# A transformer layer's differential attention: softmaxes combined unnormalized, the head norm's squares in one float32 product, the gate guard on GpSimd

## The chip, the cores and the metric

One core of one Trainium2 chip runs the whole layer. The metric is the device time of one execution in microseconds. Five engines work side by side, each on its own queue in order: the tensor engine (PE, its weight loads PEld), VectorE (DVE), ScalarE (ACT), GpSimd (POOL) and the queue that issues the transfers (SP).

## The reference

One layer for one sequence of 1024 tokens with 1024 features, all in float32. Its parts that matter here are these.

```python
proj = h @ w_in                       # queries, keys, values, latents, gate path g
p_d = jax.nn.softmax(logit_d, axis=-1)            # 4 heads, two softmaxes each
attn_d = p_d[:, 0] - lam * p_d[:, 1]
o_d = jnp.einsum('bhqk,bkhd->bqhd', attn_d, dv)
o_d = _rms_norm(o_d, diff_sub_norm) * (1.0 - lam_init)   # over the 128 values of a head
out = (mixed * jax.nn.silu(g)) @ w_out
return x + gate[:, None, :] * out
```

The four differential heads subtract a second softmax, times a scalar lambda, from the first, and normalize the result per head by its mean square plus an eps of 1e-6. Four more heads are ordinary softmax attention (MLA). Attention is causal by chunks of 64 tokens. The concatenated heads are multiplied by silu of the gate path before the output projection.

## The kernel before, in words

The kernel keeps float32 accuracy on the tensor engine by splitting each operand into a high part in a reduced-precision float32 format and a low remainder, and adding three products (`mm3`, lines 61 to 65). It runs in stages: a prologue that normalizes and transposes x, the projections (about 70 to 290 us), the mixing of both kinds of attention (about 290 to 612 us) and the output projection.

The mixing, `mixing` (line 1117), walks over 32 steps, one per head and pair of query tiles of 128 rows: 16 differential ones (`d`), 16 MLA ones (`m`), with the last differential and first MLA steps interleaved. A step first makes the softmax tiles of its pair (`diff_probs`, line 1032) and then, one step behind, the transposes, the product with the values and the output of the pair before (`diff_out`, line 1056). The head norm of that output (`diff_norm`, line 1070) is put off to the next step. Between them gate tiles fill the tensor engine (`gate_tile`, line 790): six at the start of step 0 and one in each of steps 0 to 9, 16 in all. Each is 24 matmuls of 512 columns into one PSUM bank; then VectorE clamps it from below (798), ScalarE takes exp, log of one plus it and exp again (799 to 801), VectorE multiplies by the tile (802) and SP stores it to DRAM (803).

In `diff_probs` each query tile has two score tiles. VectorE evicts the negated scores from PSUM with their running minimum (`scores`, 962), ScalarE takes the exponentials with their row sums (972). VectorE inverts both sums (1049) and multiplies the second by minus lambda (1050), GpSimd scales the second tile (1051), and VectorE scales the first and adds the second (1052). The blended tile is transposed (1019), split into high and low parts on ScalarE and VectorE (1020, 1021) and multiplied with the values (63 to 65).

In `diff_out` ScalarE copies the product (1060) and squares it in reduced precision (1063), GpSimd squares it in float32 (1066) and takes the difference to ScalarE's (1067). In `diff_norm` two matmuls with a matrix of ones sum both over the 128 values (1077), ScalarE takes log and exp for the inverse root (1079, 1080), VectorE scales (1081), GpSimd multiplies by the gate tile, which is loaded from DRAM (1074, 1082), and ScalarE and GpSimd split the result (1083, 1085) for the store (1087).

The order of each engine's instructions isn't written out in the mixing: a planner with a cost model of its own orders them by priority when the program is built, and adds the semaphores. Loads of weights and values are also split into high and low parts on ScalarE and on VectorE or GpSimd (785, 786, 877, 878). Line 939 is a small memset on GpSimd in the MLA steps, line 824 a float32 product with ones in the projections.

## Time and profile before

| | us |
|---|---|
| median of 3 runs | 677.12 (676.3 to 678.02) |
| profiled execution, its own time | 675.18 |
| its span, first to last instruction | 673.2 |
| tensor engine busy | 636.0 |

The profile is one execution recorded by the hardware. Times in it count from the span's start. A busy time is the union of an engine's instructions; a matmul's end is modelled, so the streaming of matmuls shows in the distance of their starts. The idle time before an instruction is put down to the one that released it.

### The profile page before, as it was taken

What the parts mean: (1) busy time and instruction counts of PE and PEld (TensorE: products, weight loads), DVE (VectorE), ACT (ScalarE), POOL (GpSimd) and SP (SyncE); (2) the same over time, 40 slices, a digit from 0 to 9 for tenths busy, and PEclk for the clock granted to TensorE, in tenths of its full rate; (3) what the DMA queues carried; (4) which work ended last, traced back from release to release, by engine and by line L of the source; (5) the groups of instructions that cost most, each with busy time, mean ns of one, the idle gap of its engine ahead of it and who ended that gap; (6) DMA issues with size and microseconds to landing.
All of it is one profiled execution on the core that took longest, in us unless ns stands there. A gap on an engine that the chain in (4) does not pass through costs nothing.

```text
span 673.2 us, 11178 instructions
## 1 busy us (share of the span) xinstructions
PE 636.0 (94%) x3579; PEld 538.7 (80%) x3579; DVE 480.0 (71%) x1296; ACT 341.3 (51%) x820; POOL 282.5 (42%) x376
## 2 busy tenths in 40 slices
PE   6899998999999999989999989997999899999996
PEld 4578886878888888877888878886988788888885
DVE  5855899699987554635876867989976466367654
ACT  4433663744565344345766766877775344236200
POOL 2022415483355135304443544558655225349400
PEclk9999999999999999999999998998999999999999
DMA  9984152598657455499556385493365944514223
GB/s 323 304 203 127 41 172 58 148 286 263 185 144 217 120 162 148 133 237 291 139 151 188 98 241 132 137 289 123 95 188 169 300 144 134 148 46 126 80 111 113
DMA packets 115140, 112.97 MB, mean 168 GB/s; under 512 B 7712, under 2 KB 86614, under 8 KB 115072
## 3 DMA queue, kind: packets, MB, share of 16 engines
q1 hardware_dynamic: 114784, 112.12, 57.4%
q8 instruction: 30, 0.49, 0.3%
q14 instruction: 38, 0.31, 0.2%
q0 software_dynamic: 288, 0.05, 0.1%
HBM read 77.51 MB, written 34.62 MB: 167 GB/s over the span
## 4 chain that ended last, share of the span: by engine, by line
PE 62%; DVE 14%; DMA 11%; issue 4%; ACT 3%; POOL 3%; SPq 2%; DVEq 0%; POOLq 0%; ACTq 0%
PE lg L953 8%; PE u L63 7%; PE u L65 7%; PE u L64 7%; PE o L65 4%; PE o L63 4%; PE o L64 4%; PE pt L1019 3%; DVE p L962 3%; DMA raw<-mk_d 2%; PE acc L64 2%; PE acc L65 2%; PE acc L63 2%; PE u L392 2%; DMA dk<-dk_d 2%
## 5 line engine op out<-in xcount | busy, mean ns | idle before, releaser
L972 ACT ACTIVATE p<-p,mx 128x128 f32<-128x128 f32 (+7 forms) x96 | 74.3, 775 | 35.4 <-DVE p L967 19.2
L63 PE MATMUL u<-wh,hTh 128*128 128x512 f32 x192 | 75.8, 398 | 3.3 <-DVE xn L561 2.6
L65 PE MATMUL u<-wh,hTl 128*128 128x512 f32 x192 | 76.3, 397 | 0.0
L64 PE MATMUL u<-wl,hTh 128*128 128x512 f32 x192 | 75.7, 394 | 0.0
L962 DVE TENSOR_SCALAR_CACHE_REDUCE p<-lg 128x512 f32<-128x512 f32 (+5 forms) x96 | 52.6, 563 | 13.3 <-PE pt L1019 4.5
L953 PE MATMUL lg<-dk,dq 128*128 128x512 f32 (+2 forms) x192 | 52.2, 368 | 5.6 <-DVE p L962 3.3
L535 POOL TENSOR_TENSOR wl<-wraw,wh 128x512 fp32r<-128x512 f32 (+1 forms) x20 | 26.5, 1329 | 65.4 <-ACT wh L534 60.7
L63 PE MATMUL u<-hTh,wh 128*128 128x512 f32 x128 | 51.5, 402 | 0.0
L65 PE MATMUL u<-hTh,wl 128*128 128x512 f32 x128 | 51.0, 399 | 0.0
L64 PE MATMUL u<-hTl,wh 128*128 128x512 f32 x128 | 50.5, 394 | 0.0
L1019 PE MATMUL pt<-ident_r,p 128*128 128x128 f32 x288 | 45.9, 276 | 3.4 <-DVE pTl L1021 1.7
L63 PEld LDWEIGHTS u<-wh,hTh 128*128 128x128 f32 x192 | 36.1, 188 | 10.6 <-DVE xn L561 3.3
L65 PEld LDWEIGHTS u<-wh,hTl 128*128 128x128 f32 x192 | 36.1, 188 | 7.2 <-issue 0.4
L64 PEld LDWEIGHTS u<-wl,hTh 128*128 128x128 f32 x192 | 36.1, 188 | 6.7
L953 PEld LDWEIGHTS lg<-dk,dq 128*128 128x128 f32 x192 | 31.4, 195 | 11.3 <-DVE p L962 6.1
L1021 DVE TENSOR_TENSOR pTl<-pt,pTh 128x512 fp32r<-128x512 f32 x48 | 32.9, 688 | 10.6 <-ACT pTh L1020 10.2
L1107 POOL TENSOR_SCALAR p<-p,sm 128x128 f32<-128x128 f32 (+7 forms) x32 | 25.7, 806 | 34.7 <-DVE sm L1106 34.1
L1052 DVE SCALAR_TENSOR_TENSOR p<-p,sm,p 128x128 f32<-128x128 f32 (+7 forms) x32 | 33.1, 1040 | 9.7 <-POOL p L1051 9.7
L1019 PEld LDWEIGHTS pt<-ident_r,p 128*128 128x128 f32 x288 | 34.2, 141 | 6.4 <-DVE p L1052 2.5
L1020 ACT CAST pTh<-pt 128x512 fp32r<-128x512 f32 x48 | 27.5, 581 | 21.0 <-PE pt L1019 20.6
L1051 POOL TENSOR_SCALAR p<-p,sm 128x128 f32<-128x128 f32 (+7 forms) x32 | 25.5, 797 | 27.6 <-DVE sm L1050 10.6
L953 PE MATMUL lg<-mkh,mq 128*128 128x512 f32 (+2 forms) x96 | 34.0, 365 | 0.7 <-ACT mq L877 0.7
(321 smaller groups left out, 1913.8 us busy)
## 6 DMA issues: line engine op xcount, KB each, us to landing
wraw<-in_w_in_dram SPq DMA_DIRECT2D x40, 256.0 KB, 3.4
ada<-in_ada_w_dram SPq DMA_DIRECT2D x32, 256.0 KB, 6.6
dq<-dq_d SPq DMA_DIRECT2D x16, 512.0 KB, 6.9
xt<-in_x_dram SPq DMA_DIRECT2D x8, 512.0 KB
dk_d<-st SPq DMA_DIRECT2D x16, 256.0 KB
adag<-in_ada_w_dram SPq DMA_DIRECT2D x16, 256.0 KB
dq_d<-st SPq DMA_DIRECT2D x16, 256.0 KB, 3.1
sg_d<-sgt SPq DMA_DIRECT2D x16, 256.0 KB, 4.7
```

What stands on the lines that cost most here:

```text
L63: t.matmul(out, wh, xh, start=start, stop=False)
L64: t.matmul(out, wh, xl, start=False, stop=False)
L65: t.matmul(out, wl, xh, start=False, stop=stop)
L535: (nc.gpsimd if pool else nc.vector).tensor_tensor(l, raw, h.bitcast(F32), op=ALU.subtract)
L953: self.last_mm = nc.tensor.matmul(lg[:, :w], q, k, start=j == 0, stop=j == len(ops) - 1 and not add)
L962: nc.vector.tensor_scalar(o[:, :m], lg[:, :m], 1.0, mx if c0 else None, op0=ALU.mult, op1=ALU.min, accum_out=mx)
L972: nc.scalar.activation(p, p, AF.Exp, bias=mx, scale=-1.0, accum_out=sm)
L1019: nc.tensor.transpose(t[:, j * P : j * P + P], ptiles[e[1]][:, e[0] * P : e[0] * P + P], self.ident)
L1020: nc.scalar.copy(h[:, lo:512], t[:, lo:512])
L1021: nc.vector.tensor_tensor(l[:, lo:512], t[:, lo:512], h[:, lo:512].bitcast(F32), op=ALU.subtract)
L1052: v.scalar_tensor_tensor(pp[0], pp[0], sm[:, 0:1], pp[1], op0=ALU.mult, op1=ALU.add)
L1107: nc.gpsimd.tensor_scalar(p, p, sm[:, 0:1], 0.0, op0=ALU.mult, op1=ALU.add)
```

## The change

It changes three places. In the gate tile VectorE's clamp from below goes; ScalarE takes the first exponential straight from PSUM, and GpSimd clamps the exponential from above before the log. In the softmax blend the tiles stay unnormalized: the first tile is no longer scaled, and the second is scaled by minus lambda times the ratio of the sums within VectorE's blend; GpSimd's scaling of the tile goes, and GpSimd writes the squared first sum times 128 eps into one column. In the head norm ScalarE's squares stay in float32; GpSimd builds two diagonal matrices of those columns (128x128 each), adds them to the squares, and one float32 product with ones takes the place of the two reduced-precision ones, so that eps is scaled by the squared sum; the log no longer adds eps.

```diff
--- before.py
+++ after.py
@@ -31,7 +31,7 @@
 W1 = 7
 MID = 4
 BANKS = {"a": 2, "b": 3, "c": 2, "t": 1}
-GMIN = -88.0
+EMAX = 1.6e38
 FIRST = "acactc"
 FILL = (1, 1, 1, 1, 1, 1, 1, 1, 1, 1, 0, 0)
 STAGES = {"st": 2, "mst": 3}
@@ -795,8 +795,8 @@
             hi, lo = unit[k // 4]
             self.mm3(t, hi[:, k % 4], lo[:, k % 4], self.hTh[:, k, ts], self.hTl[q][k], k == 0, k == KT - 1)
         st = self.wp.tile([P, 512], F32, name="sgt", tag="wraw", bufs=WRAW)
-        v.tensor_scalar(st, t, GMIN, None, op0=ALU.max)
-        a.activation(st, st, AF.Exp, scale=-1.0)
+        a.activation(st, t, AF.Exp, scale=-1.0)
+        self.nc.gpsimd.tensor_scalar(st, st, EMAX, 0.0, op0=ALU.min, op1=ALU.max)
         a.activation(st, st, AF.Ln, bias=self.ones[:, 0:1])
         a.activation(st, st, AF.Exp, scale=-1.0)
         v.tensor_tensor(st, st, t, op=ALU.mult)
@@ -1030,9 +1030,11 @@
         return acc[:, 0:256]
 
     def diff_probs(self, opnd, h, pr):
+
         nc, v, ap = self.nc, self.nc.vector, self.ap
         kT, qT, bias = opnd
         ptiles = []
+        s2 = ap.tile([P, 2], F32, name="s2", tag="s2", bufs=6)
         for j in range(2):
             i = 2 * pr + j
             klen = S if self.general else (i + 1) * P
@@ -1046,40 +1048,41 @@
                 passes = lambda c0, w: [(q[:, x], kT[c][:, c0 : c0 + w]) for x in range(2)]
                 self.scores(passes, bias, gt, p, mx[:, c : c + 1], sm[:, c : c + 1], True)
                 pp.append(p)
-            v.reciprocal(sm, sm)
-            v.tensor_tensor(sm[:, 1:2], sm[:, 1:2], self.nlam, op=ALU.mult)
-            nc.gpsimd.tensor_scalar(pp[1], pp[1], sm[:, 1:2], 0.0, op0=ALU.mult, op1=ALU.add)
-            v.scalar_tensor_tensor(pp[0], pp[0], sm[:, 0:1], pp[1], op0=ALU.mult, op1=ALU.add)
+            r = sm[:, 1:2]
+            v.reciprocal(r, r)
+            v.scalar_tensor_tensor(r, sm[:, 0:1], self.nlam, r, op0=ALU.mult, op1=ALU.mult)
+            v.scalar_tensor_tensor(pp[0], pp[1], r, pp[0], op0=ALU.mult, op1=ALU.add)
+            nc.gpsimd.tensor_scalar(s2[:, j : j + 1], sm[:, 0:1], sm[:, 0:1], P * EPS, op0=ALU.mult, op1=ALU.mult)
             ptiles.append(pp[0])
-        return ptiles
-
-    def diff_out(self, vv, h, pr, ptiles):
+        return ptiles, s2
+
+    def diff_out(self, vv, h, pr, probs):
+        ptiles, s2 = probs
         pT = self.transpose_probs(pr, ptiles)
         acc = self.av(pT, vv)
         o = self.dp.tile([P, 256], F32, name="o", tag="o", bufs=3)
         self.nc.scalar.copy(o, acc)
-        hi = self.dp.tile([P, 256], F32R, name="sqd", tag="sqd", bufs=2)
-        lo = self.dp.tile([P, 256], F32R, name="sql", tag="sql", bufs=1)
-        self.nc.scalar.activation(hi, o, AF.Square)
-        g = self.nc.gpsimd
-        sq = self.dp.tile([P, 256], F32, name="sq", tag="sq", bufs=1)
-        g.tensor_tensor(sq, o, o, op=ALU.mult)
-        g.tensor_tensor(lo, sq, hi.bitcast(F32), op=ALU.subtract)
-        return lambda: self.diff_norm(h, pr, o, hi, lo)
-
-    def diff_norm(self, h, pr, o, hi, lo):
+        sq = self.dp.tile([P, 256], F32, name="sq", tag="sq", bufs=2)
+        self.nc.scalar.activation(sq, o, AF.Square)
+        dg = self.dp.tile([P, 256], F32, name="dg", tag="dg", bufs=1)
+        for j in range(2):
+            self.nc.gpsimd.tensor_scalar(dg[:, j * P : j * P + P], self.ident, s2[:, j : j + 1], 0.0, op0=ALU.mult, op1=ALU.add)
+        self.nc.gpsimd.tensor_tensor(sq, sq, dg, op=ALU.add)
+        return lambda: self.diff_norm(h, pr, o, sq)
+
+    def diff_norm(self, h, pr, o, sq):
         nc, v, a = self.nc, self.nc.vector, self.nc.scalar
         sl = slice(pr * 256, pr * 256 + 256)
         sg = self.dp.tile([P, 256], F32, name="sgs", tag="sgs", bufs=1)
         nc.sync.dma_start(sg, self.sg_d[h][:, sl])
         ms = self.bank("c", "ms")
-        for x in (hi, lo):
-            nc.tensor.matmul(ms[:, 0:256], self.ones_r, x, start=x is hi, stop=x is lo)
+        nc.tensor.matmul(ms[:, 0:256], self.ones, sq, start=True, stop=True)
         ms = ms[:, 0:256]
-        a.activation(ms, ms, AF.Ln, bias=self.eps_t, scale=1.0 / P)
+        a.activation(ms, ms, AF.Ln, scale=1.0 / P)
         a.activation(ms, ms, AF.Exp, scale=-0.5)
         v.scalar_tensor_tensor(o, o, self.gsub[:, 0:1], ms, op0=ALU.mult, op1=ALU.mult)
         nc.gpsimd.tensor_tensor(sg, o, sg, op=ALU.mult)
+        hi = self.dp.tile([P, 256], F32R, name="sqd", tag="sqd", bufs=2)
         a.copy(hi, sg)
         hi = hi.bitcast(F32)
         nc.gpsimd.tensor_tensor(o.bitcast(F32R), sg, hi, op=ALU.subtract)
```

## Rows read from the trace of the kernel before

**Rows 1.** The page's busy time of each engine, whole span (us, share of span, instructions).

```profile
PE 636.0 (94%) x3579; PEld 538.7 (80%) x3579; DVE 480.0 (71%) x1296; ACT 341.3 (51%) x820; POOL 282.5 (42%) x376
```

**Rows 2.** Busy time by stretch: stretch, length, engines (instructions), granted clock, DMA share, GB/s.

```profile
285.00:323.00 38.00, 35.29 (x164) 29.07 (x163) 18.17 (x55) 18.66 (x39) 9.86 (x15) 0.96 0.89 248
323.00:400.00 77.00, 75.98 (x450) 66.28 (x449) 61.77 (x170) 53.36 (x127) 34.49 (x41) 1.00 0.63 168
400.00:412.00 12.00, 10.32 (x55) 8.95 (x53) 7.19 (x19) 8.01 (x21) 4.26 (x7) 0.86 0.44 134
412.00:440.00 28.00, 28.00 (x164) 24.81 (x163) 25.23 (x59) 21.27 (x47) 16.76 (x19) 1.00 0.53 143
440.00:450.00 10.00, 9.27 (x71) 8.60 (x70) 8.28 (x23) 8.25 (x22) 4.99 (x10) 1.00 1.03 301
...
450.00:485.00 35.00, 31.27 (x189) 26.91 (x188) 32.31 (x103) 27.46 (x69) 26.98 (x33) 0.95 0.46 142
...
485.00:510.00 25.00, 23.95 (x167) 21.49 (x166) 20.98 (x71) 16.60 (x40) 14.01 (x22) 1.00 0.48 138
```

**Rows 3.** The chain that ended last, shares by line: first 412 to 450, then 450 to 485 us.

```profile
by line: DVE p L962 15.0%; issue 11.0%; DVE p L1052 9.6%; POOL p L1051 8.1%; DMA sgs<-sg_d 7.4%; POOL sgs L1082 4.8%; DVE lastl L1021 3.9%; POOL o L1085 3.7%; ACT p L972 3.6%; DVE mq L878 3.4%; DVE pTl L1021 3.4%; POOL vl L878 3.3%; PE u L6
...
by line: DVE p L962 23.1%; PE lg L953 18.1%; DVE p L1052 13.0%; issue 8.4%; DVE sm L1050 4.1%; DVE pTl L1021 3.8%; PE pt L1019 3.7%; ACT p L972 3.5%; DVE o L1081 3.2%; PE lg L956 3.1%; DVE p L967 2.3%; PE acc L63 2.1%; PE acc L64 2.0%; PE a
```

**Rows 4.** Costliest groups: count | busy us, mean ns | idle us before, releasers; first two all shapes.

```profile
L1051 POOL TENSOR_SCALAR p<-p,sm 128x128 f32<-128x128 f32 (+7 forms) x32 | 25.5, 797 | 27.6 <-DVE sm L1050 10.6
L1052 DVE SCALAR_TENSOR_TENSOR p<-p,sm,p 128x128 f32<-128x128 f32 (+7 forms) x32 | 33.1, 1040 | 9.7 <-POOL p L1051 9.7
...
L1050 DVE TENSOR_TENSOR sm<-sm,nlam 128x1 f32<-128x1 f32 x32 | 8.2, 257 | 0.5
...
L1051 POOL TENSOR_SCALAR p<-p,sm 128x512 f32<-128x512 f32 x4 | 2.8, 700 | 2.4 <-ACT sgt L800 2.1 <-DVE sm L1050 0.4
...
L1051 POOL TENSOR_SCALAR p<-p,sm 128x128 f32<-128x128 f32 x4 | 2.5, 628 | 0.5 <-ACT p L972 0.2 <-DVE sm L1050 0.2
...
L939 POOL MEMSET p<- 64x64 f32 x32 | 3.8, 147 | 13.1 <-PE pt L1019 13.0
```

**Rows 5.** Timeline near 402 us, GpSimd, then VectorE: start, length, instruction, idle time before.

```profile
401.04 0.74 POOL L1082 TENSOR_TENSOR sgs<-o,sgs 128x256 f32<-128x256 f32 x1 [5.51 <-DMA sgs<-sg_d]
...
402.27 1.03 DVE L1052 SCALAR_TENSOR_TENSOR p<-p,sm,p 128x256 f32<-128x256 f32 x1 [2.57 <-POOL p L1051]
```

**Rows 6.** Line 798: shortest, median and longest ns; first and last start in us.

```profile
L798 DVE TENSOR_SCALAR sgt<-u x16: 669/682/693, 276.4 to 442.7; 128x512 f32<-128x512 f32 x16
```

**Rows 7.** Costliest groups, the head norm's lines on GpSimd and the tensor engine.

```profile
L1066 POOL TENSOR_TENSOR sq<-o 128x256 f32<-128x256 f32 x16 | 11.4, 711 | 4.0 <-ACT o L1060 3.4 <-PE lg L953 0.6
...
L1067 POOL TENSOR_TENSOR sql<-sq,sqd 128x256 fp32r<-128x256 f32 x16 | 12.5, 779 | 3.9 <-ACT sqd L1063 2.0 <-issue 1.1 <-POOL p L1051 0.2
...
L1077 PE MATMUL ms<-sqd,ones_r 128*128 128x256 f32 x16 | 5.1, 317 | 2.3 <-ACT sqd L1063 2.1
...
L1077 PE MATMUL ms<-sql,ones_r 128*128 128x256 f32 x16 | 4.9, 308 | 0.4 <-POOL sql L1067 0.4
...
L1082 POOL TENSOR_TENSOR sgs<-o,sgs 128x256 f32<-128x256 f32 x16 | 12.1, 756 | 31.8 <-DVE o L1081 17.0 <-DVE sm L1050 7.5 <-DMA sgs<-sg_d 6.8
```

**Rows 8.** The chain's piece of one 256-column matmul; then the tensor engine's timeline near 275 us.

```profile
415.07 0.12 PE acc L65
...
274.71 1.02 PE L824 MATMUL gps<-gsum,ones_r 128*128 128x512 f32 x2
275.17 0.80 PE L65 MATMUL u<-hTh,wl 128*128 128x512 f32 x1
275.80 0.46 PE L724 MATMUL kqp<-ident_r,kk 128*128 128x128 f32 x4
```

**Rows 9.** Timeline near 457 us, GpSimd, then VectorE.

```profile
456.83 1.58 POOL L878 TENSOR_TENSOR vl<-raw,vh 128x512 fp32r<-128x512 f32 x1
...
457.20 1.22 DVE L1050 TENSOR_TENSOR sm<-sm,nlam 128x1 f32<-128x1 f32 x1
```

## The prediction

> **What bounds the kernel now.** I read the page first: the tensor engine is busy for 636.0 us of a span of 673.2 us [rows 1]. A change to the other engines can therefore only win the tensor engine's idle time, or time that it spends at the lower clock. Next I read the busy time by stretch, to see where that idle time is [rows 2]. The edited lines run from 276 us (the first gate guard) to about 510 us (the last head norm). From 285 to 510 us the tensor engine is idle for 38.00 - 35.29 = 2.71 us, then 1.02, 1.68, 0.00, 0.73, 3.73 and 1.05 us: 10.9 us in all. Two stretches also show a granted clock below 1. It is 0.86 over 12 us and 0.95 over 35 us, so a part of each ran at 1.2 instead of 2.4 GHz. At half speed the work lost is 12 x 0.14 = 1.7 us and 35 x 0.05 = 1.75 us. All that can be won here is thus some 14 us.
>
> Then the chain of work that ended last, for two stretches [rows 3]. From 412 to 450 us its largest parts are VectorE's score evictions (L962, 15.0%), the blend of two softmaxes on VectorE (L1052, 9.6%) and GpSimd's scaling of the second softmax (L1051, 8.1%). From 450 to 485 us VectorE leads (L962 23.1%, L1052 13.0%, L1050 4.1%) and no GpSimd scaling is among the first lines. VectorE is busy for 32.31 of those 35 us, more than the tensor engine with 31.27. So the idle time from 440 to 485 us hangs on VectorE, which the change relieves. In the first stretch, 285 to 323 us, the chain is loads of keys, which nothing here touches, and I count none of its 2.71 us.
>
> **The change part by part.** *Softmax blend.* Each of 32 query tiles loses GpSimd's scaling (25.5 us in all) and the handover in front of VectorE's blend, before which VectorE stood idle for 9.7 us waiting for that line [rows 4]. The blend itself stays: one pass over two tiles with one scalar, as before. The reciprocal shrinks from two columns to one and the one-column product becomes a one-column three-operand product; both are instructions on a column, so zero. The worst of these waits shows what else goes: GpSimd stands 5.51 us for the load of the gate tile in front of its product (L1082), the scaling is queued behind it, and VectorE's blend of a 256-wide tile starts 2.57 us late [rows 5]. After the change VectorE no longer depends on GpSimd's queue here. What is late next is the tensor engine's norm product, whose squares still wait for ScalarE behind that same gate product.
>
> *Gate guard.* Sixteen VectorE passes of 0.682 us over 128x512 go (10.9 us), the last at 442.7 us [rows 6]. In their place GpSimd does one pass over SBUF between ScalarE's first exponential and its logarithm. The nearest row is GpSimd's scaling of a 128x512 tile, 0.700 us [rows 4], so the length of a gate's own chain stays as it is (0.70 against 0.68) and I cost it at nothing. The cover is that 10 of the 16 gates come one per step, in a bank that is wanted again only a step later. If the cover goes, the price is in the rivals, because ScalarE's logarithm now waits with the score exponentials queued behind it. The first exponential now reads PSUM itself, which other ScalarE instructions here do as well: zero.
>
> By the Trainium skill (GPSIMD Engine Reference, Engine selection), an elementwise add, multiply or max over a tile belongs on VectorE, since GpSimd is about twice as slow with two inputs and roughly at line rate with one. The guard has one input, and the trace bears out the second half: 0.700 us against 0.682 us. Were the factor of two to hold for it, each guard would take some 0.7 us longer and the sum would come out up to 16 x 0.7 = 11 us worse, had all of it reached the tensor engine.
>
> *GpSimd's own load.* Gone are 25.5 us of scalings, 11.4 us of squares and 12.5 us of differences (49.4 us) [rows 4, 7]. Added are 16 guards at 0.70 (11.2), 32 one-column products between a memset's 0.147 and the 128x128 scaling's 0.628 us [rows 4], 32 diagonals of 128x128 at up to 0.628 (20), and 16 sums of 256 columns at 0.78 (12.5). I take the small products at 0.25 (8), being nearer to the memset, and the diagonals at 0.5 (16). That is 47.7 us: GpSimd is as busy as before, only at other places.
>
> *Norm product.* Two reduced-precision matmuls of 256 columns become one float32 product. The stream of such matmuls advances 0.12 us per 256 columns, so two take 0.24 [rows 8]. The trace has float32 products with the same ones, of 512 columns: the first starts at 274.71 us, an ordinary 512-column matmul follows, and the next instruction starts at 275.80. Of those 1.09 us the ordinary one takes 2 x 0.12, the product 0.85, so 256 columns take 0.43 [rows 8]. Each norm costs the tensor engine 0.19 us more, 3.0 us for 16. The lower end is zero, if it falls into idle time. About a third of the norms lie after 440 us, where there is some, so I take 2.0 us.
>
> *Its wait.* Before, the first matmul waits for ScalarE's square and the second for GpSimd's difference. The tensor engine stood still 2.3 and 0.4 us for them [rows 7]. Now the one product waits for GpSimd's sum, which follows the square and lasts 0.78 us (L1067's length), while the old first matmul covered 0.12 of that. Where the tensor engine waited for the square it now waits up to 0.66 us more. Behind the product in its queue stand score products and transposes. Bounds: zero (the planner places the product later) and 16 x 0.66 = 10.6 us. I take 0.5 us, nearer to zero, because L1077 waited but 2.7 us in 32 matmuls. The eps on the square sum only shifts a bias from ScalarE to the diagonal: zero.
>
> **The sum.** Won: from 440 to 485 us there are 0.73 + 3.73 = 4.46 us of idle time and 1.75 us of lost clock. VectorE reaches them earlier by the three guards after 412 us (2.0 us) and by its waits on GpSimd, so I take 4.0 of 6.2. From 400 to 412 us the gate load stays, so I take 1.0 of 3.4. From 323 to 400 and 485 to 510 us I take 0.5 each of 1.02 and 1.05. That is 6.0 us won, 2.5 us paid, 3.5 us net. The profiled execution took 675.18 us (a span of 673.2 and 2.0 around it), which gives 671.7. The median of the three runs is 677.12, 1.94 above it, so on that scale I predict 673.6 us.
>
> **The rivals.** *No change.* VectorE isn't relieved, since what slows it is GpSimd. At 456.83 us GpSimd begins a 1.58 us difference, and a one-column VectorE product, usually 0.16 us, takes 1.22 us beside it [rows 9]; such products average 0.257 us [rows 4]. GpSimd's load stays at 47.7 against 49.4 us, so VectorE would keep standing still as often as before. Then only half of the 6.0 us comes, 3.0, the 2.5 us are paid, and it ends at 676.6. For it: GpSimd's load after 450 us is mostly other loads. Against it: the 9.7 us of plain waiting go in any case. The Trainium skill (SBUF — State Buffer, SBUF: two separate sides) states a rule for this: VectorE with two SBUF inputs and GpSimd take one shared port pair for whole instructions, and the other is blocked. The 1.22 us agree with it.
>
> *Slower by the guard.* GpSimd works in order and stands 31.8 us in front of L1082, 2.0 us for each of 16 norms [rows 7]. A guard queued behind one holds ScalarE's logarithm, and with it the score exponentials that feed the transposes. If 8 of the 10 later gates meet one, ScalarE stands 16 us; it is busy for 53.36 of 77 us [rows 2], so I let half reach the tensor engine: 8.0 - 3.5 = 4.5 us slower, 681.6. It decides from 5.5 us of such waits on. For it: GpSimd's queue is the one with the longest waits. Against it: those waits held VectorE before, 32 times and not 10, and cost it only 9.7 us.
>
> *Slower by the norm product.* The tensor engine waits for the sum at half of the norms: 8 x 0.66 = 5.3, and 3.0 for the product, 8.3 - 6.0 = 2.3 us slower, 679.4.
>
> **How the numbers follow.** A step of 0.3%, about 2.0 us, is what a measurement of this kernel can tell from no change. The forecast gets 0.52, no change 0.22, the guard 0.18, the norm product 0.08. So faster 0.52, same 0.22, slower 0.26. The forecast's own range is 667.5 to 675.0: at its low end some 9.6 of the 11.7 us that lie after 323 us are won and nothing is paid. For 8 in 10 the range must reach past no change and most of the slower cases: 667.5 to 681.
>
> **What would show it.** Right: no VectorE idle time in front of the blend for GpSimd; a tensor engine at 43.5 us or more of busy time in the 45 us after 440, with the clock at 1; a float32 norm product near 0.43 us; ScalarE's logarithm waiting for the guard for less than 5 us in all. Wrong: ScalarE standing for the guard and score exponentials late behind it; the tensor engine waiting for the norm's sum by several us; one-column VectorE products still at 0.26 us or more and the idle time after 440 us unchanged. The order is written by a planner that sees the new instructions, so an order shifted in stretches that no edit touches would also make it wrong.

## The result, and the profile after

The changed kernel is slower: 686.48 us median (682.74 to 693.12, 4 runs) against 676.71 us for the kernel before in the same call. The ratio is 1.0126, with a 95% interval from 1.0079 to 1.0173. The forecast was 673.6 us and its range ended at 681. The execution that was profiled is the longest of the four, 693.12 us, so its rows show about twice the loss of the medians (its span is 18.1 us above the span before, the medians differ by 9.8).

The page of the changed kernel, busy time by engine, answers to [rows 1].

```profile
PE 647.5 (94%) x3579; PEld 548.7 (79%) x3579; DVE 466.0 (67%) x1280; ACT 340.8 (49%) x820; POOL 281.6 (41%) x408
```

VectorE lost some 14 us of work, as the change meant it to, and GpSimd carries as much as before. But the tensor engine's busy time rose from 636.0 to 647.5 us. The busy time by stretch says why. Its columns are those of [rows 2]: the tensor engine, its weight loads, VectorE, ScalarE, GpSimd, then the granted clock.

```profile
285.00:323.00 38.00, 33.83 (x160) 27.62 (x159) 17.21 (x51) 18.19 (x39) 13.98 (x23) 0.96 0.96 269
323.00:400.00 77.00, 74.29 (x435) 64.33 (x434) 56.18 (x166) 51.58 (x124) 31.30 (x51) 1.00 0.59 154
400.00:412.00 12.00, 10.21 (x63) 9.48 (x62) 4.97 (x13) 6.69 (x17) 5.02 (x8) 0.86 0.37 117
412.00:440.00 28.00, 25.93 (x130) 21.44 (x129) 20.83 (x54) 19.14 (x45) 15.70 (x25) 0.94 0.49 133
440.00:450.00 10.00, 10.00 (x75) 9.48 (x74) 9.09 (x31) 8.68 (x24) 3.62 (x8) 1.00 0.80 191
450.00:485.00 35.00, 31.14 (x171) 26.15 (x170) 24.97 (x73) 22.98 (x53) 17.44 (x28) 0.95 0.48 156
485.00:510.00 25.00, 23.95 (x155) 21.22 (x155) 21.00 (x69) 18.04 (x47) 17.15 (x25) 1.00 0.62 175
510.00:545.00 35.00, 31.23 (x188) 27.96 (x188) 17.96 (x56) 16.18 (x34) 17.21 (x28) 0.93 0.72 210
545.00:612.00 67.00, 63.13 (x350) 54.77 (x349) 34.75 (x90) 23.96 (x48) 20.56 (x30) 0.94 0.42 124
```

The same view of the kernel before, for the two stretches that [rows 2] doesn't hold.

```profile
510.00:545.00 35.00, 31.84 (x190) 27.35 (x188) 15.82 (x44) 13.07 (x28) 13.23 (x20) 1.00 0.82 256
545.00:602.00 57.00, 55.82 (x314) 47.97 (x313) 34.64 (x92) 23.56 (x46) 23.29 (x30) 1.00 0.37 111
```

The mixing ends with the last score product of MLA, which begins at 612.8 us before and at 631.5 us after. The whole of it in one row each, before and after:

```profile
285.00:612.80 327.80, 312.54 (x1810) 271.01 (x1809) 231.88 (x655) 196.88 (x445) 157.64 (x203) 0.98 0.59 170
285.00:631.50 346.50, 323.21 (x1823) 279.55 (x1822) 220.23 (x642) 196.60 (x445) 156.09 (x234) 0.96 0.57 162
```

Two sums account for most of it. The tensor engine's idle time over the mixing was 10.9 + 3.2 + 1.2 = 15.3 us and is now 23.3 us, 8.0 more; behind the rows by stretch, up to the last score product, it has none in either kernel. The work lost to the lower clock, each stretch times what its granted clock lacks to 1, was 38 x 0.04 + 12 x 0.14 + 35 x 0.05 = 4.9 us. It is now 1.5 + 1.7 + 1.7 + 1.75 + 2.45 + 4.0 = 13.1 us, 8.2 more. Together 16.2 us, of the 18.7 by which the mixing ends later; the 3.0 us that the sixteen float32 norm products take more, by the prediction's own working, are about the rest. Of the 16.2 us 3.3 of idle time and 6.5 of clock, 9.8 in all, lie after 510 us, where of the edited lines only the last head norm runs (its product begins at 513.2 us). So large a part of the clock belongs to this execution alone. The mean granted clock on record is 0.979 here and 0.991 before, and 0.988, 0.984 and 0.984 for the other three, with spans of 680.9, 684.9 and 684.4 us; what it lacks to 1, times the span, is 2 to 5 us more in these than the 6.1 us before, of the 8 to 12 us by which they are longer.

The groups of the changed kernel that answer to [rows 4] and [rows 7]: VectorE, ScalarE, GpSimd, the tensor engine.

```profile
L1054 DVE SCALAR_TENSOR_TENSOR p<-p,sm,p 128x128 f32<-128x128 f32 (+7 forms) x32 | 28.3, 883 | 0.4
L1053 DVE SCALAR_TENSOR_TENSOR sm<-sm,nlam 128x1 f32<-128x1 f32 x32 | 12.3, 384 | 0.7 <-ACT p L972 0.4
...
L800 ACT ACTIVATE sgt<-sgt,ones_r 128x512 f32<-128x512 f32 x16 | 11.6, 724 | 0.7 <-POOL sgt L799 0.7
...
L1070 POOL TENSOR_TENSOR sq<-sq,dg 128x256 f32<-128x256 f32 x16 | 13.4, 840 | 12.5 <-ACT sq L1066 10.6 <-issue 1.7
...
L1069 POOL TENSOR_SCALAR dg<-ident_r,s 128x128 f32<-128x128 f32 x32 | 12.1, 389 | 1.1
...
L1055 POOL TENSOR_SCALAR s<-sm 128x1 f32<-128x1 f32 x32 | 10.2, 320 | 21.2 <-ACT p L972 20.0
...
L799 POOL TENSOR_SCALAR sgt<-sgt 128x512 f32<-128x512 f32 x16 | 10.0, 623 | 32.4 <-ACT sgt L798 32.4
...
L1079 PE MATMUL ms<-sq,ones_r 128*128 128x256 f32 x32 | 10.0, 396 | 0.0
```

Read alone, these rows look like a success. VectorE's wait in front of the blend went from 9.7 to 0.4 us, ScalarE's log waits only 0.7 us for the guard, and the tensor engine waits 0.0 us for the norm's sum. What it waits for instead is in the waits of the tensor engine from 285 to 620 us: in total, how often, the longest. First two lines of the kernel before, then the changed kernel.

```profile
PE lg L953 <- DVE p L962: 3.3, 5, 1.4
PE pt L1019 <- DVE p L1052: 1.6, 2, 0.9
...
PE lg L953 <- DVE p L962: 6.6, 9, 1.1
PE pt L1019 <- DVE p L1054: 4.8, 4, 2.7
PE lg L953 <- ACT mq L877: 3.8, 1, 3.8
PE acc L63 <- ACT lasth L1020: 2.8, 1, 2.8
```

These are ordinary handovers of the stage (evictions, casts, ScalarE's split of MLA queries), and not the edited lines but for the blend. The order of the work is no longer the same either. In the order of the tensor engine's instructions the last gate tile begins after 166 of the 192 score matmuls of the differential heads; before it was 144. The planner took the new instructions into its reckoning and sorted the engines anew: of the tensor engine's 3547 instructions that both kernels have, 3108 at most still follow each other in one common order.

### The profile page after: what moved, and what is told of

It is laid out like the page before. It is cut to its first block, busy times and chain, and to the rows that moved or that the text cites. A ratio compares the mean times of both kernels' runs of the same rounds, so it can differ in the third digit from the quotient of the medians.

```text
span 691.3 us, 11176 instructions
## 1 busy us (share of the span) xinstructions
PE 647.5 (94%) x3579; PEld 548.7 (79%) x3579; DVE 466.0 (67%) x1280; ACT 340.8 (49%) x820; POOL 281.6 (41%) x408
## 4 chain that ended last, share of the span: by engine, by line
PE 60%; DMA 14%; DVE 12%; ACT 4%; issue 4%; POOL 3%; SPq 3%; DVEq 0%; ACTq 0%; POOLq 0%
PE lg L953 7%; PE u L63 6%; PE u L65 6%; PE u L64 6%; PE o L63 4%; DMA wraw<-in_w_in_dram 4%; PE o L65 4%; PE o L64 4%; PE pt L1019 3%; DMA dq<-dq_d 3%; PE acc L63 2%; DVE p L962 2%; PE acc L64 2%; PE u L392 2%; PE acc L65 2%
## 5 line engine op out<-in xcount | busy, mean ns | idle before, releaser
L972 ACT ACTIVATE p<-p,mx 128x128 f32<-128x128 f32 (+7 forms) x96 | 74.3, 775 | 27.2 <-DVE p L967 14.3
L953 PEld LDWEIGHTS lg<-dk,dq 128*128 128x128 f32 x192 | 31.9, 196 | 13.1 <-DVE p L962 9.9
L1110 POOL TENSOR_SCALAR p<-p,sm 128x128 f32<-128x128 f32 (+7 forms) x32 | 26.7, 837 | 29.8 <-DVE sm L1109 29.7
L962 DVE TENSOR_SCALAR_CACHE_REDUCE p<-lg,mx 128x256 f32<-128x256 f32 (+6 forms) x48 | 26.1, 546 | 12.5 <-PE lg L956 9.4
L63 PE MATMUL acc<-pTh,vh 128*128 128x256 f32 x96 | 30.3, 315 | 0.6 <-ACT pTh L1020 0.6
```

The costliest lines, as they stand in the source:

```text
L63: t.matmul(out, wh, xh, start=start, stop=False)
L953: self.last_mm = nc.tensor.matmul(lg[:, :w], q, k, start=j == 0, stop=j == len(ops) - 1 and not add)
L962: nc.vector.tensor_scalar(o[:, :m], lg[:, :m], 1.0, mx if c0 else None, op0=ALU.mult, op1=ALU.min, accum_out=mx)
L972: nc.scalar.activation(p, p, AF.Exp, bias=mx, scale=-1.0, accum_out=sm)
L1110: nc.gpsimd.tensor_scalar(p, p, sm[:, 0:1], 0.0, op0=ALU.mult, op1=ALU.add)
```

## The experiments

Eighteen kernels, grouped by their question, about in the order in which they ran. The letters of the expectations are: A, the guard on GpSimd makes the gates late; B, the norm product; C or R, the planner's new order; H, ScalarE's wait within a gate's chain; S, the late load of the gate tile (1074) that stalls GpSimd; W, the new work itself. Times are medians, ratios are to the kernel before.

### The three parts alone, and the change without its guard

The guard alone:

```diff
...
-        v.tensor_scalar(st, t, GMIN, None, op0=ALU.max)
-        a.activation(st, st, AF.Exp, scale=-1.0)
+        a.activation(st, t, AF.Exp, scale=-1.0)
+        self.nc.gpsimd.tensor_scalar(st, st, EMAX, 0.0, op0=ALU.min, op1=ALU.max)
```

> The kernel before with the gate guard on GpSimd alone. Theory A (the guard is the cause: each gate's chain grows, and the gate matmuls come later in the tensor engine's order, the last one after 166 score matmuls of the 192 differential ones where it was 144): 6 to 10 us slower than before, the last gate's product on VectorE past 465 us. Theory B (the float32 norm product and its wait are the cause): within 2 us of before. Theory C (any edit shuffles the planner's order, and the time goes with the shuffle): anything, but then the other three runs scatter as much.

Measured: 685.98 us, ratio 1.0135 (1.0096 to 1.0175).

The blend alone:

```diff
-            v.reciprocal(sm, sm)
-            v.tensor_tensor(sm[:, 1:2], sm[:, 1:2], self.nlam, op=ALU.mult)
-            nc.gpsimd.tensor_scalar(pp[1], pp[1], sm[:, 1:2], 0.0, op0=ALU.mult, op1=ALU.add)
-            v.scalar_tensor_tensor(pp[0], pp[0], sm[:, 0:1], pp[1], op0=ALU.mult, op1=ALU.add)
+            r = sm[:, 1:2]
+            v.reciprocal(r, r)
+            v.scalar_tensor_tensor(r, sm[:, 0:1], self.nlam, r, op0=ALU.mult, op1=ALU.mult)
+            v.scalar_tensor_tensor(pp[0], pp[1], r, pp[0], op0=ALU.mult, op1=ALU.add)
```

> The kernel before with the softmax blend alone: unnormalized tiles, GpSimd's scaling gone, the norm as before, so eps is not scaled by the squared sum here (that part of the computation is left out). Theories A and B: 1 to 5 us faster than before, since VectorE's waits for GpSimd go (9.7 us) and nothing is added. Theory C: scatter of several us either way.

Measured: 677.31 us, ratio 1.0033 (1.0000 to 1.0065).

The float32 norm product alone, with ScalarE's squares as its input:

```diff
...
-        self.nc.scalar.activation(hi, o, AF.Square)
...
-        g.tensor_tensor(sq, o, o, op=ALU.mult)
-        g.tensor_tensor(lo, sq, hi.bitcast(F32), op=ALU.subtract)
...
+        self.nc.scalar.activation(sq, o, AF.Square)
...
-        for x in (hi, lo):
-            nc.tensor.matmul(ms[:, 0:256], self.ones_r, x, start=x is hi, stop=x is lo)
+        nc.tensor.matmul(ms[:, 0:256], self.ones, sq, start=True, stop=True)
...
```

> The kernel before with the float32 norm product alone: the squares summed in one float32 product, eps added as a bias as before, no diagonals. Theory A: 0 to 3 us slower (16 products at 0.19 us more on the tensor engine, less what falls into idle time; GpSimd loses two passes of each norm). Theory B: 5 us slower or more. Theory C: scatter.

Measured: 685.25 us, ratio 1.0107 (1.0078 to 1.0135).

The change with VectorE's clamp in place of GpSimd's guard (the first diff, undone in the changed kernel):

> The changed kernel with the gate guard back on VectorE. Theory A: 8 to 12 us faster than the changed kernel, that is from 3 us faster than before to 1 us slower; the last gate's product on VectorE near 446 us again. Theory B: still 5 to 10 us slower than before. Theory C: scatter.

Measured: 678.29 us, ratio 1.0051 (1.0014 to 1.0087).

By these four, the guard costs 10.5 us over before and 8.2 us within the change (measured in different calls), and the norm product 9.8 us over before. But the norm product costs next to nothing where the blend stands beside it (678.29 against 677.31). Its group in the kernel with the norm product alone shows no price of that size: the sixteen products are some 3.0 us longer, and the tensor engine waits 0.5 us in front of them.

```profile
L1071 PE MATMUL ms<-sq,ones_r 128*128 128x256 f32 x32 | 9.9, 389 | 0.5 <-ACT sq L1062 0.5
```

So the parts don't add up, and this kernel lost 9.8 us with hardly a wait at the edited place.

### The place of the guard, and the late gate load

The kernel before without any clamp:

```diff
...
-        v.tensor_scalar(st, t, GMIN, None, op0=ALU.max)
-        a.activation(st, st, AF.Exp, scale=-1.0)
+        a.activation(st, t, AF.Exp, scale=-1.0)
```

> The kernel before without any gate guard: ScalarE takes the exponential straight from PSUM and the clamp is left out. In the tensor engine's order the last gate starts after 124 score matmuls (144 before, 166 with the guard on GpSimd). Theory A (the GpSimd hop inside the gate's chain makes the planner place the gates later, so that the last differential steps run without filler): 1 to 4 us faster than before. Theory R (any step away from the order of before costs): 3 us slower or more.

Measured: 683.56 us, ratio 1.0112 (1.0068 to 1.0155). VectorE is busy for 9.1 us less (470.9 against 480.0), and the kernel is slower.

VectorE's clamp moved behind the first exponential, as a minimum of 1.6e38 on the exponential (the first diff with `v` in place of `self.nc.gpsimd`):

> The kernel before with the guard in its new place, after the first exponential, but on VectorE. The chain has the same handovers as with GpSimd (ScalarE, other engine, ScalarE), and the planner puts the last gate after 138 score matmuls. Theory A: within 3 us of before, against some 10 us with GpSimd. Theory H (it is ScalarE's wait for a second engine in mid chain that costs, whichever engine): 7 us slower or more. Theory R: 3 us slower or more.

Measured: 683.85 us, ratio 1.0079 (1.0039 to 1.0119).

Two buffers for the gate tile of the norm in the changed kernel, and one for the squares:

```diff
-        sq = self.dp.tile([P, 256], F32, name="sq", tag="sq", bufs=2)
+        sq = self.dp.tile([P, 256], F32, name="sq", tag="sq", bufs=1)
...
-        sg = self.dp.tile([P, 256], F32, name="sgs", tag="sgs", bufs=1)
+        sg = self.dp.tile([P, 256], F32, name="sgs", tag="sgs", bufs=2)
```

> The changed kernel with two buffers instead of one for the gate tile that the head norm loads (and one instead of two for its squares, for room); the tensor engine's gate positions are the same as in the changed kernel. Theory S (GpSimd standing for the late gate load holds ScalarE and then the tensor engine, and the clock falls after that): 4 to 8 us faster than the changed kernel. Theory A alone: within 2 us of the changed kernel.

Measured: 683.91 us, ratio 1.0115 (1.0069 to 1.0160).

The same edit in the change without its guard:

> The changed kernel with the guard back on VectorE and two buffers for the gate tile that the head norm loads. Theory S: 2 to 5 us faster than the same kernel with one buffer (678.3 us), so as fast as before or faster. Theory A alone: within 2 us of 678.3.

Measured: 679.06 us, ratio 1.0030 (0.9998 to 1.0063).

A and H fall as full accounts, since the kernel with no guard at all is also 1.1% slower. S expected 4 to 8 us; it finds 2.6 us by the medians (686.48 to 683.91, measured in different calls), 0.1% by the ratios (1.0126 to 1.0115), and nothing in the change without its guard (678.29 to 679.06).

The changed kernel with two buffers also shows an execution nearer to the medians. Its tensor engine has the changed kernel's order but for two instructions, its profiled execution took 683.8 us, and its last score product begins at 622.2 us.

```profile
285.00:622.20 337.20, 317.58 (x1822) 274.39 (x1821) 220.14 (x642) 196.52 (x445) 157.37 (x234) 0.98 0.57 167
```

The tensor engine is idle for 19.6 us of the mixing, 4.3 more than before, and by the granted clock of 0.988 over a span of 682.0 us the clock costs 8.2 us, 2.1 more. With the 3.0 us of the longer norm products that is 9.4 us, by which its mixing ends later.

### The order by itself

Two kernels that do the same work as before, with a detail exchanged that gives the planner another order. First, the second softmax of a pair is made first:

```diff
...
-            for c in range(2):
+            for c in (1, 0):
...
```

> The kernel before with the second softmax of each query tile made ahead of the first: the same instructions, the same durations, another order by the planner (the tensor engine's list differs in 3676 lines; gate positions 142 against 144). Theory R (the order of before is a good one among many, and any new order costs): 0.3% to 1% slower (2 to 7 us). Theory A and every theory that puts the loss on an instruction: within 0.3% of before.

Measured: 688.53 us, ratio 1.0207 (1.0172 to 1.0243).

Second, VectorE and GpSimd are exchanged in the split of the gate weights (786), which they share in halves:

```diff
-            (nc.vector if b else nc.gpsimd).tensor_tensor(lo, raw, hi.bitcast(F32), op=ALU.subtract)
+            (nc.gpsimd if b else nc.vector).tensor_tensor(lo, raw, hi.bitcast(F32), op=ALU.subtract)
```

> The kernel before with VectorE and GpSimd exchanged in the split of the gate's two weight halves: the same number of instructions on each engine, another order by the planner (2481 lines on the tensor engine; the last gate after 148 score matmuls). Theory R: 0.3% to 1% slower. Theories that put the loss on an instruction of the change: within 0.3% of before.

Measured: 682.73 us, ratio 1.0120 (1.0085 to 1.0156).

The guard on top of the second one:

> The reordered kernel p8 with the gate guard on GpSimd. A cost of the guard itself shows again over p8, 8 to 10 us as in the two pairs so far (10.5 over before, 8.2 over the changed kernel with the guard on VectorE). Theory R alone: no slower than p8 by more than 4 us, or any amount.

Measured: 682.03 us, ratio 1.0129 (1.0087 to 1.0171).

The changed kernel with the score matmuls of a step queued behind the gate three steps earlier, which moves the last gate back to 144 score matmuls:

```diff
...
+                    if n - 3 in pins and k == "d":
+                        c.enter_context(self.tc.issue_after(pins[n - 3].ins))
...
```

> The changed kernel, with each gate's matmuls held in front of the score matmuls three steps on, so that the last gate starts after 144 score matmuls as before, not 166. If the late gates are what the guard costs: 5 to 9 us faster than the changed kernel. If it is not the place of the gates: within 3 us of the changed kernel.

Measured: 693.98 us, ratio 1.0267 (1.0224 to 1.0309).

A new order with no change of work costs 1.2% or 2.1% in these two, as much as the whole change or more. VectorE is busy for 482.8 and 479.7 us in them and GpSimd for 282.7 and 285.6, against 480.0 and 282.5 before. The longest waits of the tensor engine in the kernel with the softmaxes exchanged (285 to 620 us) are for VectorE's evictions, as in the changed kernel, and for the gate's product on VectorE that frees a bank.

```profile
PE lg L953 <- DVE p L962: 7.3, 6, 3.9
PE u L63 <- DVE sgt L802: 4.1, 3, 3.2
```

The guard's 10.5 us over before are nothing on top of a kernel whose order is another one already (682.73 to 682.03 us, ratios 1.0120 and 1.0129). The place of the gates alone isn't it either: put back, the kernel becomes slower still (693.98 against 686.48), which neither expectation had.

### The work at an equal order

What these runs leave out is the work at an equal order. So the next kernels carry a list of every engine's instructions in the order of another kernel, and hold it:

```diff
...
+        if not self.general:
+            self.hold_order()
...
+    def hold_order(self):
+        at = {i.name: i for i in self.nc.cur_bb.bb.instructions}
+        for names in HELD.values():
+            last = None
+            for n in names:
+                i = at.get(f"I-{n}")
...
+                    self.tc.add_manual_dep(
+                        i,
+                        last.name,
+                        mybir.DependencyInfo(mybir.DependencyClass.NoSync, mybir.DependencyReason.DATA),
+                        reason="order",
+                    )
+                last = i
```

Such an edge fixes the order in which an engine issues and adds no wait. In the traces the instructions that a held kernel shares with the one whose order it holds stand in that order on the tensor engine, VectorE and GpSimd, all of them. No run of the kernel before held to its own order is on record; that holding costs little rests on the blend alone, held, at 0.9988. `HELD` names all instructions that both kernels have; what the other kernel lacks is placed by the planner or stands where its counterpart stood, as each expectation says.

The changed kernel in the order of before:

> The changed kernel with every engine held in the order that the planner gave the kernel before (only the 16 norm products on the tensor engine and the 16 guards on GpSimd are placed by the planner; the squares' diagonals and sums stand where GpSimd's squares and differences stood). Theory R (the loss is the planner's new order): the work of the change is worth what the prediction said of it or nothing, so 671 to 677 us, ratio 0.992 to 1.001. Theory W (the new work itself costs: the guard, the float32 product, the waits for the sum): 683 to 689 us, ratio 1.010 or more. In between, 678 to 682, both have a part.

Measured: 699.79 us, ratio 1.0334 (1.0285 to 1.0384).

The same without the guard:

> The same with VectorE's clamp in place of GpSimd's guard, so the blend and the norm product alone in the order of before. Theory R: 673 to 678 us, ratio 0.995 to 1.002, and within 2 us of the run with the guard in that order. Theory A (the guard costs by itself): 4 us or more below that run.

Measured: 685.82 us, ratio 1.0134 (1.0092 to 1.0176).

The kernel before in the order of the changed kernel:

> The other way round: the kernel before with every engine held in the order that the planner gave the changed kernel (VectorE's clamps and three operations of the blend, GpSimd's scalings, squares and differences and the two norm products placed by the planner). Theory R: as slow as the changed kernel or slower, 684 to 692 us, ratio 1.010 to 1.023. Theory W: 675 to 680 us, ratio under 1.005.

Measured: 705.50 us, ratio 1.0415 (1.0374 to 1.0456).

The changed kernel, with the halves exchanged, in the order that these halves give the kernel before:

> The changed kernel with VectorE and GpSimd exchanged in the split of the gate weights, held in the order that the planner gave the kernel before with that exchange (682.73 us, ratio 1.0120). Theory R: what the change is worth at an equal order is the same here as in the order of before, so 677 to 683 us, ratio 1.003 to 1.012. Theory W: 690 us or more, ratio over 1.02.

Measured: 692.60 us, ratio 1.0239 (1.0189 to 1.0289); over the 682.73 us of that order (measured in another call), 1.4%, or 1.2% by the ratios.

The blend alone in the order of before:

> The kernel before with the unnormalized blend alone (GpSimd's 32 scalings gone, eps not scaled by the squared sum), every instruction of every engine held in the order of before. This is the forecast's term 'won 6.0 us' by itself. If the wait taken from VectorE reaches the tensor engine as the prediction had it: 668 to 673 us, ratio 0.987 to 0.994. If it is hidden anyway: 675 to 679 us, ratio 0.997 to 1.003. If the blend itself costs (theory W): 681 or more.

Measured: 674.69 us (12 runs), ratio 0.9988 (0.9960 to 1.0016).

The guard alone in the order of before:

> The kernel before with GpSimd's guard alone, every engine held in the order of before, the guards placed by the planner. By the difference of the two held runs (699.79 with the guard, 685.82 without) the guard costs 14 us in this order: 688 to 694 us, ratio 1.015 to 1.025, with ScalarE standing 12 to 20 us in front of the log for the guard (17.2 us there). If that price came only together with the other two edits: 676 to 682 us.

Measured: 681.79 us, ratio 1.0114 (1.0068 to 1.0161).

R falls as the only cause: at an equal order the change costs 3.3% in the order of before, and 1.2 to 1.4% in the other. W falls as the only cause too, since unchanged work in the changed kernel's order is slower still, by 4.2%. Both exchanges of order came out slower than either theory had them. Each of the two orders fits the work that it was made for better than the other's. With the order held, waits stand at the edited places. First the guard: the group of ScalarE's log (800 in the plain kernels), in the guard alone.

```profile
L807 ACT ACTIVATE sgt<-sgt,ones_r 128x512 f32<-128x512 f32 x16 | 11.6, 722 | 12.4 <-POOL sgt L806 12.3
```

And in the whole change, held, with the group of the norm product:

```profile
L807 ACT ACTIVATE sgt<-sgt,ones_r 128x512 f32<-128x512 f32 x16 | 11.6, 722 | 17.2 <-POOL sgt L806 17.2
...
L1086 PE MATMUL ms<-sq,ones_r 128*128 128x256 f32 x32 | 13.3, 506 | 14.3 <-POOL sq L1077 14.3
```

ScalarE stands 12.4 or 17.2 us in front of the log for the guard; in the kernel before, that line waits 0.3 us. It costs 6.4 us alone (675.40 to 681.79) and 14.0 us in the whole (685.82 to 699.79), so about half of its price there comes only beside the other edits. The worst stand in the guard alone, first GpSimd, then ScalarE, shows what the guard waits behind: GpSimd's other work, a split of values and the norm's last difference.

```profile
432.95 1.28 POOL L885 TENSOR_TENSOR vl<-raw,vh 128x512 fp32r<-128x512 f32 x1
434.19 1.46 POOL L1092 TENSOR_TENSOR o<-sgs,sqd 128x256 fp32r<-128x256 f32 x1
...
436.27 0.72 ACT L807 ACTIVATE sgt<-sgt,ones_r 128x512 f32<-128x512 f32 x1 [3.24 <-POOL sgt L806]
```

Next the norm product, in the run without the guard:

```profile
L1086 PE MATMUL ms<-sq,ones_r 128*128 128x256 f32 x32 | 10.7, 415 | 11.2 <-POOL sq L1077 11.2
```

The tensor engine stands 11.2 us for GpSimd's sum, and the ratio rises from 0.9988 with the blend alone to 1.0134 with the norm beside it. How much of such waits becomes idle time of the tensor engine is in the rows from 285 us to the last score product: the blend alone, the guard alone, the change without its guard, the whole change, all held.

```profile
285.00:615.00 330.00, 310.26 (x1806) 269.79 (x1805) 227.63 (x650) 197.06 (x445) 131.40 (x170) 0.98 0.59 168
285.00:618.40 333.40, 311.62 (x1807) 270.21 (x1806) 223.06 (x640) 195.55 (x444) 165.52 (x217) 0.98 0.58 166
285.00:619.80 334.80, 311.01 (x1814) 270.12 (x1813) 228.62 (x654) 197.14 (x445) 144.14 (x219) 0.99 0.58 167
285.00:638.70 353.70, 321.92 (x1809) 278.86 (x1808) 220.51 (x640) 195.78 (x444) 154.65 (x234) 0.96 0.55 157
```

It is 19.7, 21.8, 23.8 and 31.8 us, against 15.3 before. The guard alone adds 6.5 us and the blend with the norm 8.5, which is about what the two cost by their medians (6.4 and 8.0). The blend alone adds 4.4 us though it costs nothing; its profiled execution is 3.5 us above its median, so one profile is good to a few us only. The guard on top of the other two adds 8.0 us of idle time and, by the granted clocks on record (0.994 and 0.976) times the spans, 12.7 us of clock, between two profiles 18.4 us apart.

Last the blend, by the waits of VectorE from 323 to 510 us. First the kernel before:

```profile
DVE p L1052 <- POOL p L1051: 8.9, 9, 2.6
DVE sgt L798 <- PE u L65: 4.4, 4, 3.0
DVE pTl L1021 <- ACT pTh L1020: 2.8, 7, 0.7
```

Then the blend alone in its order, where the lines stand 7 further down (805 and 1028 are 798 and 1021):

```profile
DVE sgt L805 <- PE u L72: 8.4, 7, 3.4
DVE pTl L1028 <- ACT pTh L1027: 7.1, 8, 4.0
```

The 8.9 us for GpSimd are gone, and the waits for the gate matmuls (4.4 to 8.4) and for ScalarE's cast (2.8 to 7.1) have grown by 8.3 us. VectorE came earlier and waited for the tensor engine and for ScalarE instead. The stretch that the forecast counted on didn't fill either, as that kernel's busy time by stretch shows:

```profile
440.00:450.00 10.00, 8.74 (x67) 8.13 (x65) 6.78 (x25) 6.69 (x19) 3.67 (x5) 1.00 0.98 329
450.00:485.00 35.00, 30.07 (x169) 26.16 (x170) 30.84 (x94) 26.64 (x68) 20.97 (x28) 0.90 0.37 112
```

The tensor engine is busy there for 38.8 of 45 us, against 9.27 + 31.27 = 40.5 before [rows 2].

## Why the prediction was wrong

**What bounds the kernel: right.** The tensor engine does, and what a change of the other engines can move is its idle time and its clock. Both moved upwards, by 8 us each in the profiled execution and by 4.3 and 2.1 us in the one nearer to the medians; there the longer norm products are a third part. Two of the readings in its working are off without touching the sum. Three stretches of [rows 2] have a clock below 1 and not two, but the third, at 0.96, is the one that it counted at nothing. And for the guard to decide, 5.5 us had to reach the tensor engine, which at a half is 11 us of standing.

**The 6.0 us won by VectorE's relief: the first step that failed.** The prediction said that "the idle time from 440 to 485 us hangs on VectorE, which the change relieves", and took 4.0 us there. The relief came (9.7 to 0.4 us), and three of the four signs of being right with it (0.4 us, 0.43 us, 0.7 us); the fourth, on the tensor engine itself, failed: 41.1 us of the 45 and a clock of 0.95. At an equal order the blend is worth 0.7 us (0.9988, interval 0.9960 to 1.0016, so 2.7 us at most). The three guards after 412 us, 2.0 us of the reckoning, stay on VectorE in that run; without any clamp, in an order of its own, the kernel is 1.1% slower. A share of the chain of waits was taken for a price: VectorE led that chain, but in the order of before the wait taken from it was followed in its queue by waits for ScalarE and for the tensor engine that took up the time.

**The norm product: the product right, its wait wrong.** It takes 0.43 us as worked out. In the changed kernel's timeline (start, length) the product begins at 332.33 us and the second matmul behind it at 332.88. One ordinary matmul of 0.12 lies between, so 0.43 are left.

```profile
332.33 0.59 PE L1079 MATMUL ms<-sq,ones_r 128*128 128x256 f32 x2
332.57 0.47 PE L63 MATMUL acc<-pTh,vh 128*128 128x256 f32 x1
332.88 0.28 PE L64 MATMUL acc<-pTl,vh 128*128 128x256 f32 x1
```

For the wait the prediction had bounds of zero and 10.6 us and took 0.5. Both ends occur: 0.0 us in the changed kernel, whose planner puts the product later (a median of 0.8 us behind the sum, where the held kernels have 0.05), and in the order of before 11.2 us without the guard and 14.3 with it, past the upper bound. A held order with the product placed later wasn't run.

**The guard at nothing: failed.** The guard itself is as short as the row of before said, 0.623 us against an estimate of 0.70. By the Trainium skill (GPSIMD Engine Reference, Engine selection) GpSimd is roughly at line rate with one input. The 0.682 us beside which the prediction set it is VectorE's clamp from PSUM; the same operation on the exponential in SBUF is shorter on VectorE, by the kernel with the clamp moved (second line), a median of 0.426 us against GpSimd's 0.614, so there the trace has GpSimd 1.4 times as long.

```profile
L799 POOL TENSOR_SCALAR sgt<-sgt x16: 612/614/758, 279.1 to 466.2; 128x512 f32<-128x512 f32 x16
...
L799 DVE TENSOR_SCALAR sgt<-sgt x16: 414/426/987, 275.5 to 437.9; 128x512 f32<-128x512 f32 x16
```

What it costs in the order of before is the way there and back in the middle of ScalarE's queue. The rival "slower by the guard" had ScalarE standing 16 us, with half reaching the tensor engine. It stands 12.4 to 17.2 us, and 6.4 to 14.0 us reach the end. The rival's reason was another one, though: with the guard alone, none of the 16 guards stands behind GpSimd's wait in front of the gate product (L1082); where one stands, it is behind GpSimd's work. This rival had a chance of 0.18. In the planner's own order ScalarE waits 0.7 us, and there the guard's price isn't shown apart from the order's.

**The step behind all three.** Each term was worked out in the order of before. The prediction named the order last, as something that "would also make it wrong", and gave it neither a chance nor a price. The planner did sort anew, and in its order the three places look well (0.4, 0.7 and 0.0 us). By the two kernels of equal work, a new order of this kernel can cost 1.2 to 2.1%. Not every one does: the blend alone and the change without its guard ran in new orders too, at 1.0033 and 1.0051. Still no other order tried here is better than that of before, and the changed kernel gave it up to get past waits that cost 3.3% where it is kept. How much of the 1.26% is then order and how much is work stays open, because an order held for one kernel's work puts the other's in bad places. No version found here beats the kernel before; the best, the blend alone in its order, can't be told from it.

## What to carry to other kernels

Where a planner orders the engines, price a change twice: at the order that stands, and with what a new order of the same work costs, measured by exchanging a detail that changes no work. A wait taken from an engine counts as a gain only if the next thing in that engine's queue is ready; look for what it waits for next. Moving a short operation from VectorE to GpSimd in the middle of a ScalarE chain is no free trade: in the order of before, ScalarE stood 12.4 us for 16 such operations, and 6.4 us reached the end.

## What the runs showed of the hardware

In the changed kernel the granted clock fell behind several stalls of the tensor engine, and such a stall cost more than its own length. The busy time by stretch around the stall at 537 us (2.85 us in front of a matmul that waits for ScalarE's cast) shows it:

```profile
530.00:540.00 10.00, 7.50 (x38) 6.01 (x36) 3.27 (x13) 3.66 (x7) 4.20 (x7) 1.00 0.95 302
540.00:547.00 7.00, 6.66 (x25) 6.03 (x26) 3.13 (x6) 2.88 (x6) 2.73 (x4) 0.52 1.01 277
547.00:560.00 13.00, 13.00 (x82) 11.72 (x81) 8.62 (x26) 4.81 (x11) 1.11 (x4) 1.00 0.52 186
```

From 540 to 547 us the clock is 0.52, so nearly all of it ran at 1.2 instead of 2.4 GHz though the engine was busy for 6.66 of 7 us. A stall of 2.85 us took another 7 x 0.48 = 3.4 us behind it. Not every stall does: one of 1.81 us ends at 106.97 us, and from 100 to 115 us the clock is 1.00. And a three-operand product on one column is longer than the plain one, whose difference the prediction had costed at zero: a median of 0.220 us against 0.160, 1.9 us of VectorE's time in 32. The means, 0.384 against 0.257 us [rows 4], differ by more because a few of them take up to 1.3 us in either kernel; with the blend alone, held, the mean of the same product is 0.268.
